# A decoder layer in fp32: the first softmax sum of a differential head moved into the RMS norm's factor, and the sliding pairs' values moved behind their transposes

## The chip, the cores and the metric

The kernel runs on one core of a Trainium2 chip. The metric is the device time of one execution in microseconds (us), as a median over runs. The engines are named as in the profile: PE is TensorE (PEld its weight loads), DVE VectorE, ACT ScalarE, POOL GpSimd, and SP is SyncE, which issues most of the DMAs. A line such as L766 is line 766 of the kernel before.

## What is computed

One layer, width 1024, 512 tokens, all in fp32. A conditioned RMS norm and one input projection feed two causal mixers side by side: sliding-window attention (8 heads, a sink per head) and differential attention (4 heads). Each mixer is projected to the width, gated and merged; an output projection, a second norm, a gated MLP with a short convolution and a final norm follow. The change touches the two mixers:

```python
# differential attention, one block of 128 queries
p = jax.nn.softmax(scores, axis=-1)
a = p[:, :, 0] - lam * p[:, :, 1]
out = jnp.einsum('bhqs,bshe->bqhe', a.astype(v.dtype), v)
...
out = _rmsnorm(out, subln_g) * (1.0 - lam_init)

# sliding window: softmax over 256 keys and one sink, then the values
probs = jax.nn.softmax(jnp.concatenate([scores, sink], axis=-1), axis=-1)[..., :-1]
out = jnp.einsum('bnkgqs,bnskd->bnqkgd', probs.astype(v.dtype), vb)
```

## The kernel before, in words

**Products.** An fp32 matrix product is made of three matmuls on operands split in a high and a low part (mm3, L121 to L124). Whoever makes an operand casts the high part on ScalarE and subtracts it on VectorE to get the low part (evac, L490 and L491, or with a scale L493 and L494; for weights split, L118 and L119).

**Stages.** Up to about 56 us the input projection of the sliding heads; then the sliding heads to about 111 us; the differential heads with the first gates to about 215; more gates and the merge to about 310; then the output projection and the MLP (L1260, L1875) to the end.

**Fills.** While softmax work runs on VectorE and ScalarE, TensorE is kept busy with *fill* steps (L539): each takes one k-step, three matmuls of 128x512, of the next unit in a list. The units are the q, k and v projections of the differential heads (add_head, L679), and the gates and branch projections. Their weights are loaded by SyncE two units ahead (load_cols, L519) into four shared "raw" buffers. The values of a differential head are transposed on TensorE in a turn that comes V_LAG = 13 fills after their projection (pv, L703).

**The w_ada rows.** In the same raw buffers VectorE sums up rows of the conditioning matrix: loads of 512 KB (ada_load, L828), each multiplied and added by two L852 (the first of a row by L850) into arow, and every 8th fill takes one more step of it (ada_rows, L832). For two of these steps (ROW_BEHIND) the sum may only be issued behind the division of a given sliding pair. A finished row is spread over the partitions by TensorE (pr, L869).

**PSUM.** Eight banks: two "f" for the projections, three "s" for scores, two "t" for transposes and anything short (tp, td, pv, pr, pss, rb, and the values oa of sliding pairs 0, 1 and 3), one "v" (oa of pair 2, the od of differential heads, some score tiles). The t bank goes in turns, so whoever takes one waits until the last but one user has been read.

**Order.** TensorE's order is the program's (a manual schedule). The order on VectorE and ScalarE is found by a scheduler from priorities (high_priority) and "issue after" conditions, before the program runs; at run time each engine then works strictly in its order.

**Sliding pairs.** Two heads are worked together (i and i+4): four pairs. Per pass of the loop at L928: SWA_FILL[3] = 2 fills; the values of pair i−1 (swa_values, L661) and the scores of pair i+1; the transposes of pair i for head j=0, first half (four, tile tp), one fill, second half (three), one fill; those for j=1 (seven in a row); two fills; the softmax of pair i+1 (L620 to L644); five fills. The values of pairs 2 and 3 come behind the loop.

**Differential heads.** A loop over 16 steps s, one per head and block of 128 queries: fills, scores of two steps ahead (sd, L742), transposes of the finished step (diff_transpose, td, L778), softmax of the two steps ahead (diff_softmax, L749), and behind each head its values (diff_values, od) and statistics. In the softmax ScalarE makes the exponentials of both maps and their sums (L760); VectorE takes the reciprocals (L763), multiplies the second with −lambda (L764), scales the second map by it (L765) and adds the first map scaled by its own reciprocal (L766). From od the squares are summed over channels by TensorE (pss, L801), the norm's factor is made (rstd_m2, L178 to L195), turned by a transpose (rb, L808) and multiplied in, NORM_LAG = 16 fills later for the last head and in a later step for the others.

Of the kernel before, what the change touches and what calls it, by code (L numbers as in the profile page):

```python
# [8 lines left out]
F32 = mybir.dt.float32  # L9
F32R = mybir.dt.float32r  # L10
AF = mybir.ActivationFunctionType
ALU = mybir.AluOpType
PSUM = bass.MemoryType.PSUM

P = 128
# [3 lines left out]
NT = S // P  # L19
# [19 lines left out]
SWA_FILL = (2, 2, 5, 2, 2, 2, 2, 3)  # L39
DIFF_FILL = (3, 2, 4, 2)  # L40
# [14 lines left out]
def kernel(  # L55
# [22 lines left out]
    nc = tc.nc  # L78
# [21 lines left out]
    def tbank(name, shape=(P, S)):  # L100
        return bank("t", 2, list(shape), name)

    def vbank(name):
        return bank("v", 1, [P, S], name)
# [92 lines left out]
    def rstd_m2(dst, ssq, n, d, wpool, plus=None):  # L197
        rstd_end(dst, *rstd_start(ssq, n, d, wpool, plus), n, wpool)
# [242 lines left out]
    for gi in range(KT):  # L441
# [4 lines left out]
        else:  # L446
            h_low(gi)
            lp = cpool.tile([P, 2, 64], F32, name="lp")
            ls = cpool.tile([P, 2], F32, name="ls")
            nlam = cpool.tile([P, 1], F32, name="nlam")  # L450
# [31 lines left out]
    ap = pool("att", stack=at)  # L482
# [56 lines left out]
    def fill(n):  # L539
        for _ in range(n):  # L540
            if not current:
                prefetch()
                if loaded:
                    wts, run = loaded.pop(0)
                    current.append(run(wts))
                    if tick[0]:
                        prefetch()
            if tick[0] == 7:
                prefetch()
            if current:  # L550
                try:
                    next(current[0])
                except StopIteration:
                    current.clear()
            for e in list(later):
                e[0] -= 1
                if e[0] <= 0:
                    later.remove(e)
                    e[1]()
            tick[0] += 1  # L560
            if tick[0] >= ADA_START and tick[0] % ADA_EVERY == 0:
                next(ada, None)
# [6 lines left out]
    def flush(*kinds):  # L569
        for kind in kinds:  # L570
            while beside[kind]:
                beside[kind].pop(0)()
# [70 lines left out]
                    sb = c.sb[n][:, j, :w]  # L643
                    c.divided = nc.vector.tensor_scalar_mul(sb, sb, c.lsum[:, j, n : n + 1])  # L644

    def swa_transpose(i, j, halves=(0, 1)):
        c = pairs[i]
        if 0 in halves:
            c.pT.append(ap.tile([P, 1024], F32, tag="aTh" if j == 0 else "aTl", bufs=2, name=f"pT{i}_{j}"))
        pt = c.pT[j]  # L650
        for b in halves:
            wb = 512 if b == 0 else 384
            tp = tbank(f"tp{i}_{j}_{b}")
            for m in range(wb // P):
                kb, n = 2 * b + m // 2, 2 * b + m // 2 + m % 2
                off = (kb - max(0, n - 1)) * P
                nc.tensor.transpose(tp[:, m * P : (m + 1) * P], c.sb[n][:, j, off : off + P], ident)
            with tc.high_priority(offset=HP):
                c.copied = nc.scalar.copy(pt[:, b * 512 : b * 512 + wb], tp[:, :wb])

    def swa_values(i):  # L661
        o = vbank(f"oa{i}") if i == 2 else tbank(f"oa{i}")
        for kb in (0, 2, 1, 3):
            w = P if kb == 3 else 2 * P
            for j in range(2):
                rows = slice(64 * j, 64 * j + 64)
                nc.tensor.matmul(
                    o[rows, kb * P : kb * P + w], va[:, kb, rows],
                    pairs[i].pT[j][:, kb * 256 : kb * 256 + w],
                    start=kb == 0, stop=kb == 3, tile_position=(0, 64 * j),  # L670
                )

        with tc.high_priority(offset=HP), tc.issue_after(pairs[3].divided.ins) if i == 2 else ExitStack():
            evac(outa[0][:, i], outa[1][:, i], o)
# [74 lines left out]
    def diff_softmax(*ss):  # L749
        with tc.high_priority(offset=HP):  # L750
            for s in ss:
                nc.vector.tensor_scalar_mul(scored[s][0], scored[s][0], -(2.0 ** (-2 * (s // NT + 1))))  # L752
            behind = ExitStack()
            for s in ss:
                h, n = divmod(s, NT)
                slope = 2.0 ** (-2 * (h + 1))
                mx, pm = scored[s]
                lsum = ap.tile([P, 2], F32, tag="dls", bufs=3, name=f"dls{h}_{n}")
                for m in range(2):
                    exp = nc.scalar.activation(  # L760
                        pm[m], pm[m], AF.Exp, bias=mx[:, m : m + 1], scale=slope, accum_out=lsum[:, m : m + 1]
                    )
                nc.vector.reciprocal(lsum, lsum)  # L763
                nc.vector.tensor_mul(lsum[:, 1:2], lsum[:, 1:2], nlam)  # L764
                nc.vector.tensor_scalar_mul(pm[1], pm[1], lsum[:, 1:2])  # L765
                last = nc.vector.scalar_tensor_tensor(pm[0], pm[0], lsum[:, 0:1], pm[1], ALU.mult, ALU.add)  # L766
                probs[s] = pm[0]
                behind.enter_context(tc.issue_after(exp.ins))
                behind.enter_context(tc.issue_after(last.ins))
            behind.close()  # L770
# [12 lines left out]
    def diff_values(h):  # L783
        t, (aTh, aTl) = heads[h], aTs[h]
        o = vbank(f"od{h}")
        for k in range(NT):
            q0 = k * P
            mm3(
                o[:, q0:], t[:, 4, k * P : (k + 1) * P], t[:, 5, k * P : (k + 1) * P],
                aTh[:, k * AW + q0 : k * AW + 512], aTl[:, k * AW + q0 : k * AW + 512],  # L790
                k == 0, k == NT - 1,
            )
        sq = ap.tile([P, S], F32, tag="tmp", bufs=2, name=f"sq{h}")
        of = ap.tile([P, S], F32, tag="of", bufs=2, name=f"of{h}")
        nc.scalar.activation(sq, o, AF.Square)
        nc.scalar.activation(of, o, AF.Copy, scale=sublnc)

        def stats():
            pss = tbank(f"pss{h}", (P, NT))
            for n in range(NT):  # L800
                nc.tensor.matmul(pss[:, n : n + 1], sq[:, n * P : (n + 1) * P], ones[:, 0:1], start=True, stop=True)  # L801
            rs = ap.tile([P, NT], F32, tag="drs", bufs=2, name=f"drs{h}")
            rstd_m2(rs, pss, NT, P, ap)

            def turn_norm():
                rb = tbank(f"rb{h}")
                for n in range(NT):
                    nc.tensor.transpose(rb[:, n * P : (n + 1) * P], rs[:, n : n + 1].to_broadcast([P, P]), ident)  # L808
                nc.vector.tensor_mul(of, of, rb)
                split(outd[0][:, h], outd[1][:, h], of)  # L810

            if h < 3:
                beside["norm"].append(turn_norm)
            else:
                after(NORM_LAG, turn_norm)

        if h < 3:
            beside["sum"].append(stats)
        else:
            after(STAT_LAG, stats)  # L820
# [86 lines left out]
        units.append((lambda: load_cols(win, COL_GA + j * P, f"wga{j}"), gate))  # L907
        units.append((load, branch))

    group_ahead = [1]  # L910
    pairs, firsts, scored, probs, aTs = {}, {}, {}, {}, {}
    ada = ada_rows()
    add_head(0)
# [14 lines left out]
    for i in range(SWA_PAIRS):  # L928
        more = i + 1 < SWA_PAIRS
        fill(SWA_FILL[3])  # L930
        if more:
            flush("row")
            if i:
                swa_values(i - 1)
            swa_scores(i + 1, range(NT))
        swa_transpose(i, 0, (0,))
        fill(1)
        swa_transpose(i, 0, (1,))
        fill(SWA_FILL[4] - 1)
        swa_transpose(i, 1)  # L940
        fill(SWA_FILL[5])
        if more:
            with tc.issue_after(pairs[i].copied.ins):
                swa_softmax(i + 1)
        fill(SWA_FILL[6] + SWA_FILL[7])
    while units or loaded or current:
        fill(1)
    flush("row")
# [9 lines left out]
    fill(DIFF_FILL[0])  # L958
    for s in range(4 * DIFF_HEADS):
        h, n = divmod(s, NT)  # L960
        if n == 0 and 0 < h < 3:
            add_head(h + 1)
        elif s == 12:
            add_gate_a(2)
            add_gate_a(3)
        fill(DIFF_FILL[1])
        nxt = (s + 1, s + 2) if n % 2 and s < 15 else ()
        if nxt:
            flush("row")
            diff_scores(*nxt)  # L970
        if n == 1:
            diff_transpose(s)
        fill(DIFF_FILL[2])
        if n == 2:
            flush("sum")
        elif n == 0:
            flush("norm")
        if n != 1:
            diff_transpose(s)
        if s == 13:  # L980
            group_ahead.clear()
        elif s > 13:
            flush("row")
        diff_softmax(*nxt)
        if n == 0 and h:
            diff_values(h - 1)
            fill(DIFF_FILL[3])
# [334 lines left out]
    ssq, r2, xns = {}, {}, {}  # L1322
# [608 lines left out]
```

## Time and profile before

| | us |
|---|---|
| median of 3 runs | 693.56 (693.17 to 693.79) |
| the profiled execution's own time | 693.12 |
| its span in the trace | 691.1 |
| TensorE busy | 679.9 of 691.1 |
| VectorE busy | 567.8 |
| ScalarE busy | 383.9 |

All groups of lines below are of the profiled execution, in us from the start of its span. Busy time is a sum over stages; what an engine's wait is worth is read where it stands, in the timeline. In a timeline row stand the start, the length, the engine, the line, the operation, what it writes and reads, the shapes and how many of them follow each other; a bracket gives the idle time before the row and who ended it. Rows of TensorE overlap: matmuls are pipelined.

### The profile page before, as it was taken

Reading aid. Unit: us, or ns where it says so; the run is one execution under the profiler, and the core shown is the slowest. Engines: PE = TensorE matmul, PEld = TensorE weight load, DVE = VectorE, ACT = ScalarE, POOL = GpSimd, SP = SyncE. Lnnn points to the kernel's source line nnn. Section 1 sums busy time; section 2 is a strip of 40 time slices with the busy share of each in tenths; the row PEclk is TensorE's granted clock in tenths of the full one; section 3 lists DMA queues with packets and bytes.
Section 4 is the critical chain, followed back from the end, with each engine's and each line's share of the span. In section 5 each row is a group of like instructions: output and inputs, shape, how many; then the busy total and the mean of one; then the engine's idle time right before and its main releaser. Section 6 shows DMA issues by size and latency. Waiting matters only on the chain.

```text
span 691.1 us, 11254 instructions
## 1 busy us (share of the span) xinstructions
PE 679.9 (98%) x4203; PEld 592.9 (86%) x4203; DVE 567.8 (82%) x1073; ACT 383.9 (56%) x686; POOL 83.3 (12%) x100
## 2 busy tenths in 40 slices
PE   8999999999999999999999999999999999999995
PEld 5887787778888888888899999999999999888884
DVE  4999996987985666663789988888888999979997
ACT  6676675445552323332477756655565666656665
POOL 3000000000101000000030101112111002540300
PEclk9999999999999999999999999999999999999998
DMA  9985454553456675229725788777889648996903
GB/s 304 350 241 178 151 156 126 154 159 97 140 143 181 195 219 178 91 96 308 236 60 125 169 211 199 164 174 215 189 227 223 155 155 202 193 203 193 167 1 121
DMA packets 115926, 121.81 MB, mean 176 GB/s; under 512 B 4447, under 2 KB 93344, under 8 KB 115872
## 3 DMA queue, kind: packets, MB, share of 16 engines
q1 hardware_dynamic: 96958, 95.09, 43.3%
q0 software_dynamic: 18720, 25.73, 21.9%
q8 instruction: 33, 0.54, 0.3%
q10 hardware_dynamic: 194, 0.28, 0.1%
q14 instruction: 21, 0.17, 0.1%
HBM read 118.97 MB, written 2.11 MB: 175 GB/s over the span
## 4 chain that ended last, share of the span: by engine, by line
PE 89%; DVE 5%; DMA 3%; issue 1%; ACT 1%; SPq 0%; POOLq 0%; ACTq 0%
PE up L1260 32%; PE dc L1875 15%; PE a L385 5%; DMA ra<-in_w_ada_dram 2%; PE pgd L122 2%; PE oc L1316 2%; PE oc L1320 2%; PE pgd L124 2%; PE oc L1317 2%; PE pgd L123 2%; PE pga L122 2%; PE pga L124 2%; PE pga L123 2%; DVE arow L852 1%; PE pB L122 1%; PE pB L123 1%
## 5 line engine op out<-in xcount | busy, mean ns | idle before, releaser
L1260 PE MATMUL up<-t,m_whi 128*128 128x256 f32 x512 | 93.1, 283 | 0.0
L1260 PEld LDWEIGHTS up<-t,m_whi 128*128 128x128 f32 x512 | 79.9, 192 | 0.0
L1260 PE MATMUL up<-t,m_wlo 128*128 128x256 f32 x256 | 72.4, 283 | 0.0
L1260 PE MATMUL up<-bh,p_whi 128*128 128x256 f32 x232 | 65.7, 283 | 0.0
L1260 PE MATMUL up<-bl,p_whi 128*128 128x256 f32 x232 | 65.7, 283 | 0.0
L1260 PE MATMUL up<-bh,p_wlo 128*128 128x256 f32 x232 | 65.7, 283 | 0.0
L852 DVE SCALAR_TENSOR_TENSOR arow<-ra,cs,arow 128x512 f32<-128x512 f32 x56 | 41.9, 749 | 14.9 <-DMA ra<-in_w_ada_dram 14.2
L1260 PEld LDWEIGHTS up<-t,m_wlo 128*128 128x128 f32 x256 | 49.2, 192 | 0.0
L1260 PEld LDWEIGHTS up<-bh,p_whi 128*128 128x128 f32 x232 | 44.5, 192 | 0.0
L1260 PEld LDWEIGHTS up<-bl,p_whi 128*128 128x128 f32 x232 | 44.5, 192 | 0.0
L1260 PEld LDWEIGHTS up<-bh,p_wlo 128*128 128x128 f32 x232 | 44.5, 192 | 0.0
L1169 POOL DMA_DIRECT2D s<-in_w_up_dram x21 | 27.1, 1366 | 141.0 <-DMA s<-in_w_up_dram 62.9
L1197 ACT CAST m_whi<-s 128x1024 fp32r<-128x1024 f32 x31 | 32.4, 1047 | 11.1 <-DVE s L1191 7.7
L1201 DVE TENSOR_TENSOR m_wlo<-s,m_whi 128x1024 fp32r<-128x1024 f32 x31 | 37.7, 1217 | 0.0
L1260 PE MATMUL up<-t,p_whi 128*128 128x256 f32 x176 | 32.2, 283 | 0.0
L875 POOL DMA_DIRECT2D mod_rows<-row x8 | 5.0, 622 | 207.1 <-ACT row L874 207.1
L185 POOL TENSOR_TENSOR r<-ms,mhalf 128x1 f32<-128x1 f32 (+1 forms) x16 | 13.8, 865 | 117.2 <-DVE ms L183 72.9
L1260 PEld LDWEIGHTS up<-t,p_whi 128*128 128x128 f32 x176 | 27.5, 192 | 0.0
L1267 ACT ACTIVATE gT<-a,cv 128x512 f32<-128x512 f32 x22 | 17.7, 813 | 16.9 <-DVE a L1302 15.8
L1197 ACT CAST p_whi<-wa 128x1024 fp32r<-128x1024 f32 x18 | 18.8, 1042 | 12.6 <-PE up L1260 12.6
L760 ACT ACTIVATE sd<-sd,dmx 128x128 f32<-128x128 f32 (+3 forms) x32 | 17.6, 554 | 13.5 <-DVE dmx L752 13.3
L1201 DVE TENSOR_TENSOR p_wlo<-wa,p_whi 128x1024 fp32r<-128x1024 f32 x18 | 22.0, 1221 | 3.8 <-ACT p_whi L1197 3.8
(488 smaller groups left out, 2074.4 us busy)
## 6 DMA issues: line engine op xcount, KB each, us to landing
ra<-in_w_ada_dram SPq DMA_DIRECT2D x32, 512.0 KB, 3.7
wa<-in_w_up_dram SPq DMA_DIRECT2D x22, 512.0 KB, 4.2
s<-in_w_up_dram SPq DMA_DIRECT2D x21, 512.0 KB, 4.7
s<-in_w_up_dram POOLq DMA_DIRECT2D x21, 512.0 KB, 7.2
adaw<-in_w_ada_dram SPq DMA_DIRECT2D x12, 512.0 KB, 7.0
w<-in_w_in_dram SPq DMA_DIRECT2D x12, 512.0 KB, 4.7
a<-in_w_up_dram SPq DMA_DIRECT2D x11, 512.0 KB, 4.5
b<-in_w_down_dram SPq DMA_DIRECT2D x10, 512.0 KB, 5.3
```

The costliest lines, as they stand in the source:

```text
L122: nc.tensor.matmul(o, lh, rh, start=start, stop=False)
L123: nc.tensor.matmul(o, lh, rl, start=False, stop=False)
L124: nc.tensor.matmul(o, ll, rh, start=False, stop=stop)
L385: nc.tensor.matmul(acc6[i], lhs[:, i * P : (i + 1) * P], rhs[k], start=k == 0 and p == 0, stop=last and p == 2)
L760: exp = nc.scalar.activation(pm[m], pm[m], AF.Exp, bias=mx[:, m : m + 1], scale=slope, accum_out=lsum[:, m : m + 1])
L852: nc.vector.scalar_tensor_tensor(ac, r[:, a], cc, ac, ALU.mult, ALU.add)
L1169: nc.gpsimd.dma_start(dst, upblock(*blk), accum_op=ALU.add)
L1197: nc.scalar.copy(W[J, name][0], R[J, SRC[name]])
L1201: nc.vector.tensor_sub(lo, R[J, SRC[name]], hi.bitcast(F32))
L1260: nc.tensor.matmul(o[u], w[:, k, cu], b[:, k], start=name in ("p1", "m5", "p2") and k == 0 and x == 0, stop=k == 3 and x == 2, skip_group_ ...
L1267: nc.scalar.activation(grow(j), av[J][:, u], AF.Identity, bias=cv[:, 66 + j : 67 + j], scale=cv[:, 44 + j : 45 + j])
L1875: nc.tensor.matmul(bank2[u][:, sl], a[:, q, cu], b[:, q, sl], start=first_mm and x == 0, stop=last_mm and x == 2, skip_group_check=name no ...
```

## The change

Four things.

1. swa_transpose does both halves of a head at once. For j=0 the fill that stood between the halves now stands behind them.
2. The values of pairs 0 and 1 are taken in their own pair's pass, behind SWA_FILL[6] = 2 fills that follow the transposes, and no longer ahead of the next pass's scores: five fills earlier. All values but those of pair 3 use the v bank.
3. The differential softmax no longer divides by the first map's sum. With s0 and s1 the sums of the two maps, it makes e0 + (−lambda·s0/s1)·e1, which is s0 times what it made before. The sixteen L765 go, L763 and L764 act on one column, and L766 reads the same two maps. What is left of s0 goes into the norm's factor: with r = 1/s0 the sum of squares is multiplied by r² ahead of the norm's epsilon, and the factor by r. These are four operations on 128x4 per head. The sums of a head's four blocks are kept in one tile for that.
4. In step s = 1 of the differential loop one fill moves from ahead of the scores and the transposes to behind them. (The condition at add_head is written anew and means the same.)

The loads, their order on SyncE and the number of matmuls stay.

```diff
-    def swa_transpose(i, j, halves=(0, 1)):
+    def swa_transpose(i, j):
         c = pairs[i]
-        if 0 in halves:
-            c.pT.append(ap.tile([P, 1024], F32, tag="aTh" if j == 0 else "aTl", bufs=2, name=f"pT{i}_{j}"))
-        pt = c.pT[j]
-        for b in halves:
+        pt = ap.tile([P, 1024], F32, tag="aTh" if j == 0 else "aTl", bufs=2, name=f"pT{i}_{j}")
+        c.pT.append(pt)
+        for b in range(2):
...
     def swa_values(i):
-        o = vbank(f"oa{i}") if i == 2 else tbank(f"oa{i}")
+        o = tbank(f"oa{i}") if i == 3 else vbank(f"oa{i}")
...
-                lsum = ap.tile([P, 2], F32, tag="dls", bufs=3, name=f"dls{h}_{n}")
-                for m in range(2):
+                if n == 0:
+                    sums[h] = ap.tile([P, 2, NT], F32, tag="dls", bufs=2, name=f"dls{h}")
+                ls0, ls1 = (sums[h][:, m, n : n + 1] for m in range(2))
+                for m, ls in enumerate((ls0, ls1)):
                     exp = nc.scalar.activation(
-                        pm[m], pm[m], AF.Exp, bias=mx[:, m : m + 1], scale=slope, accum_out=lsum[:, m : m + 1]
+                        pm[m], pm[m], AF.Exp, bias=mx[:, m : m + 1], scale=slope, accum_out=ls
                     )
-                nc.vector.reciprocal(lsum, lsum)
-                nc.vector.tensor_mul(lsum[:, 1:2], lsum[:, 1:2], nlam)
-                nc.vector.tensor_scalar_mul(pm[1], pm[1], lsum[:, 1:2])
-                last = nc.vector.scalar_tensor_tensor(pm[0], pm[0], lsum[:, 0:1], pm[1], ALU.mult, ALU.add)
+                nc.vector.reciprocal(ls1, ls1)
+                nc.vector.scalar_tensor_tensor(ls1, ls1, ls0, nlam, ALU.mult, ALU.mult)
+                last = nc.vector.scalar_tensor_tensor(pm[0], pm[1], ls1, pm[0], ALU.mult, ALU.add)
...
-            rs = ap.tile([P, NT], F32, tag="drs", bufs=2, name=f"drs{h}")
-            rstd_m2(rs, pss, NT, P, ap)
+            rs, r0, r2 = (ap.tile([P, NT], F32, tag=t, bufs=2, name=f"{t}{h}") for t in ("drs", "dr0", "dr2"))
+            nc.vector.reciprocal(r0, sums[h][:, 0])
+            nc.vector.tensor_mul(r2, r0, r0)
+            nc.vector.tensor_mul(r2, r2, pss)
+            rstd_m2(rs, r2, NT, P, ap)
+            nc.vector.tensor_mul(rs, rs, r0)
...
         if more:
             flush("row")
-            if i:
-                swa_values(i - 1)
             swa_scores(i + 1, range(NT))
-        swa_transpose(i, 0, (0,))
-        fill(1)
-        swa_transpose(i, 0, (1,))
-        fill(SWA_FILL[4] - 1)
+        swa_transpose(i, 0)
+        fill(SWA_FILL[4])
         swa_transpose(i, 1)
         fill(SWA_FILL[5])
         if more:
             with tc.issue_after(pairs[i].copied.ins):
                 swa_softmax(i + 1)
-        fill(SWA_FILL[6] + SWA_FILL[7])
+        fill(SWA_FILL[6])
+        if i < 2:
+            flush("row")
+            swa_values(i)
+        fill(SWA_FILL[7])
...
-        fill(DIFF_FILL[1])
+        ahead = s == 1
+        fill(DIFF_FILL[1] - ahead)
         nxt = (s + 1, s + 2) if n % 2 and s < 15 else ()
         if nxt:
             flush("row")
             diff_scores(*nxt)
         if n == 1:
             diff_transpose(s)
-        fill(DIFF_FILL[2])
+        fill(DIFF_FILL[2] + ahead)
```

More of the change, by code (lines that the diff above doesn't have):

```diff
@@ L908, in add_gate_a @@
         units.append((load, branch))
-    group_ahead = [1]
+    group_ahead, sums = [1], {}
     pairs, firsts, scored, probs, aTs = {}, {}, {}, {}, {}
@@ L960 @@
         h, n = divmod(s, NT)
-        if n == 0 and 0 < h < 3:
+        if s in (4, 8):
             add_head(h + 1)
```

## The prediction

> **What bounds the kernel now.** I read the page first: its row of the granted clock and its chain of waits.
>
> ```profile
> PEclk9999999999999999999999999999999999999998
> ...
> PE 89%; DVE 5%; DMA 3%; issue 1%; ACT 1%; SPq 0%; POOLq 0%; ACTq 0%
> ```
>
> TensorE runs at full clock from end to end and holds 89% of the chain that ended last, so a part of this change counts only as far as it makes TensorE wait less or more. Next came the table of stretches, for the part of the program that the change touches.
>
> ```profile
> 83.00:108.00 25.00, 25.00 (x160) 20.26 (x162) 20.15 (x73) 18.12 (x54) 0.00 (x0) 1.00 0.49 147
> ```
>
> Its first pair of numbers is the stretch's length and TensorE's busy time: 25.00 of 25.00 us. There is nothing to win here, but a new wait would cost its full length. The view of TensorE's waits and its timeline then give the stalls that can be won. Here are all of them above 0.3 us between 56 and 683 us, each with the row ahead of it (columns: start, length, instruction; in brackets the idle time before it and what ended it).
>
> ```profile
> 81.28 0.40 PE L124 MATMUL pw<-hThB,w_l 128*128 128x512 f32 x1
> 82.57 0.55 PE L657 MATMUL tp<-ident,st 128*128 128x128 f32 x3 [0.89 <-DVE outal L491]
> ```
>
> ```profile
> 128.61 0.39 PE L122 MATMUL pA<-outah,wba_h 128*128 128x512 f32 x1
> 128.84 0.39 PE L123 MATMUL pA<-outal,wba_h 128*128 128x512 f32 x1
> 129.07 0.39 PE L124 MATMUL pA<-outah,wba_l 128*128 128x512 f32 x1
> 129.85 0.52 PE L778 MATMUL td<-ident,sd 128*128 128x128 f32 x3 [0.40 <-DVE dls L763]
> ...
> 138.07 0.39 PE L124 MATMUL pq<-hThA,w_l 128*128 128x512 f32 x1
> 138.81 0.30 PE L778 MATMUL td<-ident,sd 128*128 128x128 f32 x1 [0.35 <-DVE dls L763]
> ```
>
> Matmuls follow each other at 0.23 us (128.61, 128.84, 129.07), so a fill step of three takes 0.69. TensorE would have been free at 81.28 + 0.23 = 81.51, 129.30 and 138.30. The three stalls are so 1.06, 0.55 and 0.51 us; the brackets are shorter because a matmul's row overlaps the next one's. The first is tp1_0_1 waiting for a t bank that oa0 held until VectorE had made outal from it. The other two are td0_2 and td1_0 waiting for the softmax (the bracket names L763; L766, the last of that group, is what the transposes read).
>
> **The sliding pairs.** (1) oa0 moves to the v bank, so the stall before tp1_0_1 goes: −1.06 us. (2) The step that stood between the two halves of j=0 now stands behind them. That makes the second half due one fill earlier, and its t bank may not be free. For pairs 1 and 2 it is: it held transposes that ScalarE has copied long before. For pair 3 the bank of tp3_0_1 was that of pv0, the values of the first differential head behind their transposes, and it comes free only when VectorE has done L491 on pv.
>
> ```profile
> 104.69 0.49 PE L657 MATMUL tp<-ident,st 128*128 128x128 f32 x3
> ...
> 105.72 0.93 PE L657 MATMUL tp<-ident,st 128*128 128x128 f32 x7
> ```
>
> ```profile
> 91.59 1.22 DVE L119 TENSOR_TENSOR wga_l<-wga,wga_h 128x1024 fp32r<-128x1024 f32 x1
> 92.72 0.68 DVE L494 SCALAR_TENSOR_TENSOR qkv<-pq,qkv 128x512 fp32r<-128x512 f32 x1
> 93.33 0.68 DVE L491 TENSOR_TENSOR outal<-oa,outah 128x512 fp32r<-128x512 f32 x1
> 93.92 0.74 DVE L852 SCALAR_TENSOR_TENSOR arow<-ra,cs,arow 128x512 f32<-128x512 f32 x1
> 94.58 0.28 DVE L620 CUSTOM_DVE_ANT_0 st<-sw,dsw 128x128 f32<-128x128 f32 x1
> ...
> 97.07 0.36 DVE L631 TENSOR_SCALAR nm<-mx,nsink 128x4 f32<-128x4 f32 x2
> ...
> 103.36 0.69 DVE L491 TENSOR_TENSOR qkv<-pv,qkv 128x512 fp32r<-128x512 f32 x1
> ```
>
> Before, VectorE ended at 103.36 + 0.69 = 104.05, and tp3_0_1, at 104.69, didn't wait. Now TensorE comes to it 1.06 earlier by the stall that went, and 0.78 earlier by the fill that moved (1.03 from 104.69 to 105.72 holds one fill and the three transposes; a fill's first matmul behind transposes costs 0.09 more): at about 102.85. Even at before's VectorE times that is a wait of 1.2 us.
>
> And VectorE gets later, not earlier. outal of oa1 is now done long before (it was at 93.33; it fits into idle time and shifts the rest little), and the new order of VectorE's instructions puts the first L852 on ra01_4 *ahead* of wga's L119, which with L494 stood ahead of it. VectorE executes in order, so wga's L119, L494, the scores of pair 3, their softmax and L491 on pv are all queued behind a wait for that load. Its row on SyncE, the DMA view's median for the two issued between 86 and 94 us, and, for the line's four issues between 86 and 100 us, the least, median and longest from issue to landing:
>
> ```profile
> 88.53 4.67 SPq L828 DMA_DIRECT2D ra<-in_w_ada_dram  x2
> ```
>
> ```profile
> ra<-in_w_ada_dram SPq DMA_DIRECT2D x2, 512.0 KB, 4.8
> ```
>
> ```profile
> DMA to landing us min/median/max: 3.7/4.3/4.8
> ```
>
> The order of SyncE's issues and what they wait for is unchanged, and the buffer that ra01_4 takes comes free by VectorE work whose sum ahead of it is the same. So I leave its issue at 88.53 and take 4.8: landed at 93.33. VectorE would be free for it about 1.3 us sooner (my estimate: 93.92 less outal's 0.59, wga's and qkv's 1.74 and what is added ahead, about 0.5 for outal and a later sum of the softmax). From 93.33: L852 0.66 (93.92 to 94.58) gives 93.99; L119 1.13 (91.59 to 92.72) 95.12; L494 0.61, 95.73; the scores 2.49 (94.58 to 97.07), with the second L852, 0.66, now among them, 98.88. What follows on ScalarE was queued in before behind copies of the transposes:
>
> ```profile
> 97.70 0.31 ACT L632 ACTIVATE es<-nm,sink 128x4 f32<-128x4 f32 x1
> ```
>
> That is 0.63 behind VectorE's 97.07; with the copies out of the way I take VectorE's row of 0.36 instead: 99.24. From there to L491 on pv were 5.66 us (97.70 to 103.36), all of it exponentials and what hangs on them: 104.90, its 0.69, and 0.14 of signal (an L766 that ended at 129.09 + 0.62 released TensorE at 129.85; its row is below): TensorE goes on at **105.73**, a new stall of 2.9 us. From there to the next seven transposes it has 1.03 and the moved fill's 0.69: 107.45 against 105.72 before. **The sliding part: +1.73 us** (1.06 won, 2.79 lost). Its bounds are 104.05 + 0.14 + 1.72 = 105.91 (+0.2) if VectorE were no later than before, and, with a load 1.1 us slower again (4.8 less 3.7, put on top), +2.8. I take the middle, as it adds up from rows.
>
> (3) The values moved by five fills, the same 16 matmuls, and a fill's saving of 0.09 where transposes were merged against one where values now part two fills, cancel. All of it lies ahead of that stall, which absorbs up to 2.9 us; so nothing. pr00, oa2 and oa3, and the gates behind them, shift as one.
>
> **The differential heads.** Sixteen L765 go (0.42 at 384 columns). Instead each head has four operations on 128x4 (nothing above 0.36, the row of two such at 97.07; I take 0.2 each), and L764 gets a third operand at one column.
>
> ```profile
> 122.16 0.44 PE L778 MATMUL td<-ident,sd 128*128 128x128 f32 x2
> ```
>
> ```profile
> 120.65 0.35 DVE L765 TENSOR_SCALAR sd<-sd,dls 128x256 f32<-128x256 f32 x1
> 120.91 0.68 DVE L491 TENSOR_TENSOR qkv<-pv,qkv 128x512 fp32r<-128x512 f32 x1
> 121.51 0.47 DVE L766 SCALAR_TENSOR_TENSOR sd<-sd,dls,sd 128x256 f32<-128x256 f32 x1
> ...
> 128.63 0.42 DVE L765 TENSOR_SCALAR sd<-sd,dls 128x384 f32<-128x384 f32 x1
> 129.09 0.62 DVE L766 SCALAR_TENSOR_TENSOR sd<-sd,dls,sd 128x384 f32<-128x384 f32 x1
> ...
> 137.99 0.29 DVE L765 TENSOR_SCALAR sd<-sd,dls 128x128 f32<-128x128 f32 x1
> 138.31 0.35 DVE L766 SCALAR_TENSOR_TENSOR sd<-sd,dls,sd 128x128 f32<-128x128 f32 x1
> ```
>
> In before's times: td0_1 comes one fill earlier, at 122.16 − 0.69 = 121.47. L766 takes L765's place, and L491 on pv1, whose bank td0_1 needs, follows: 120.65 + 0.39 + 0.69 = 121.73, with 0.14 TensorE goes at 121.87: a new stall of 0.40, which carries to td0_2 (the fills between are one more): arrival 129.70. Its data, without L765's 0.46 (128.63 to 129.09): 129.85 − 0.46 = 129.39. So no wait; the gain is 0.15. td1_0 then arrives at 138.15. Its L766 had ended at 138.66; ahead of it three L765 go (0.46 for that of 128.63, at least as much for the next block's with 512 columns, 0.32 for its own from 137.99 to 138.31) and two of the small operations come (0.4): 138.66 − 1.24 + 0.4 + 0.14 = 137.96, no wait. The gain grows to 138.81 − 138.15 = **0.66 us**. If only its own L765 counted, 138.81 − 0.32 = 138.49 would leave a gain of 0.32; and nothing, if an exponential comes last. A fourth stall, some 0.1 us ahead of td2_2, goes too by my estimate. The final factor's two operations lengthen the path from pss to rb by 0.4 to 0.8; NORM_LAG puts 16 fills (11 us) between, which hide it.
>
> **Sum:** 1.73 − 0.66 − 0.1 = about +0.95 us on the profiled execution's 693.12, 694.07. That execution lies 0.44 under the median of 693.56, so I expect a median of **694.5**.
>
> **Rivals.**
> *The load doesn't bind.* With 3.7 us from issue to landing the chain to L491 comes 1.1 earlier, and the sum is 0.95 − 1.1 = −0.15: 693.4. Were the bank of tp3_0_1 free on time altogether, it would be 693.56 − 1.06 − 0.76 = 691.7. For it: 3.7 stands in the row; only VectorE's order, not a need of data, puts wga behind ra01_4. Against it: 4.8 is the time for that very transfer, and even before's 104.05 is 1.2 too late.
> *The differential part gives nothing (slower).* The two stalls, before td0_2 and td1_0, end where they ended before if ScalarE's exponentials, and not VectorE's operations behind them, come last. Its place is VectorE at 128.63 and 138.31, its price the 0.66, and it decides as soon as L766 ends no earlier although L765 is gone. Then only +1.73 stands: 695.3. For it: the small operations wait for the exponentials, too. Against it: L765 stands between them and L766 in the rows above.
> *A slow clock behind the new stall.* 2.9 us idle could lower the granted clock for the matmuls that follow. If it halved for as long as the idle time, half of 2.9 us would be lost: 1.45, so 694.5 + 1.45 = 696.0. It decides only if a stall of that length is long enough. The PEclk row is 9 through the stall of 1.06, which speaks against it but is shorter. [...]
> *It doesn't do what it says for the time:* bank and stall trade evenly, 693.6.
>
> **How the numbers follow.** Forecast 0.48. Load early or no net effect 0.18 (of which 0.09 at 691.7 or near). Differential part nothing, or a longer wait on the bank, 0.28. Slow clock 0.06. About 0.2%, 1.39 us, can be told from no change: 692.17 to 694.95. Faster: 0.09 and a little of the forecast's spread, 0.1. Slower: 0.28 + 0.06, 0.34, less what the differential part gives in part and more for the forecast's own spread (medians here lie within 0.3 us): 0.35. The range runs from 692.3 (between 691.7 and the early load) to 695.8 (sliding part +1.73, 0.5 more on the bank); outside stay the slow clock and most of the fully free bank.
>
> **What would show it.** In the changed profile: no idle before tp1_0_1 near 81; L852 on arow waiting for DMA ra near 92 to 93 us on VectorE; tp3_0_1 idle 2 to 3 us near 103, released by qkv's L491; td0_1 with 0.4 behind the same line; no stalls before td0_2 and td1_0. If tp3_0_1 waits less than 1 us, or if TensorE past 240 us shows idle time of its own, the forecast is wrong.

## The result, and the profile after

| | before | with the change |
|---|---|---|
| median (20 runs each) | 693.59 us | 695.38 us |
| lowest to highest | 693.04 to 695.18 | 694.03 to 698.0 |
| ratio, 95% interval | | 1.0025 (1.0017 to 1.0033) |
| profiled execution, its span | 693.12, 691.1 | 695.87, 693.8 |

The change makes the kernel 1.8 us slower. The forecast was 694.5, in a range of 692.3 to 695.8: the side and the place were right, and about half of the loss is missing. The executions also scatter twice as far as before.

TensorE's waits with the change, as total, times, longest (the change shifts the lines: L657 is now L656, L852 is L856, L828 is L832, and L764 to L766 are the three VectorE operations that are left of the softmax; in the experiments the lines shift by a few once more):

```profile
PE tp L656 <- DVE qkv L491: 2.1, 1, 2.1
...
PE td L778 <- DVE qkv L491: 0.2, 1, 0.2
```

The wait of tp on outal and the two of td on dls are gone. In their place stand two waits on L491 of qkv, both forecast. The timeline of VectorE shows where the long one is made:

```profile
91.34 1.07 DVE L644 TENSOR_SCALAR st<-st,lsum 128x128 f32<-128x128 f32 x4
93.36 0.75 DVE L856 SCALAR_TENSOR_TENSOR arow<-ra,cs,arow 128x512 f32<-128x512 f32 x1 [0.94 <-DMA ra<-in_w_ada_dram]
94.03 1.22 DVE L119 TENSOR_TENSOR wga_l<-wga,wga_h 128x1024 fp32r<-128x1024 f32 x1
...
98.91 0.36 DVE L631 TENSOR_SCALAR nm<-mx,nsink 128x4 f32<-128x4 f32 x2
...
104.87 0.68 DVE L491 TENSOR_TENSOR qkv<-pv,qkv 128x512 fp32r<-128x512 f32 x1
```

VectorE idles for 0.94 us on the load of ra01_4, with wga's product (L119) in line behind it, and comes to L491 on pv at 104.87. TensorE's timeline around that:

```profile
102.89 0.60 PE L656 MATMUL tp<-ident,st 128*128 128x128 f32 x4
105.61 0.55 PE L656 MATMUL tp<-ident,st 128*128 128x128 f32 x3 [2.12 <-DVE qkv L491]
105.92 0.48 PE L122 MATMUL pw<-hThA,w_h 128*128 128x512 f32 x1
106.23 0.59 PE L123 MATMUL pw<-hTlA,w_h 128*128 128x512 f32 x1
106.62 0.63 PE L124 MATMUL pw<-hThA,w_l 128*128 128x512 f32 x1
107.05 0.63 PE L122 MATMUL pw<-hThA,w_h 128*128 128x512 f32 x1
...
107.90 0.63 PE L124 MATMUL pw<-hThA,w_l 128*128 128x512 f32 x1
108.33 1.59 PE L656 MATMUL tp<-ident,st 128*128 128x128 f32 x7
109.67 0.48 PE L122 MATMUL pw<-hThB,w_h 128*128 128x512 f32 x1
```

Read the starts. In before, the three matmuls of a fill behind transposes start 0.32, 0.23 and 0.23 us apart. Here they start 0.31 and 0.39 us apart, from 106.62 on 0.43, and the seven transposes take 1.34 (108.33 to 109.67), where before they took 0.68 (105.72 to 106.40). After that the pace is as before. The table of stretches has the reason; its last but two column is the granted clock:

```profile
105.60:106.50 0.90, 0.89 (x5) 0.85 (x6) 0.55 (x1) 0.30 (x1) 0.00 (x0) 0.87 0.00 0
106.50:107.50 1.00, 1.00 (x4) 0.71 (x4) 0.00 (x0) 0.17 (x1) 0.00 (x0) 0.50 0.00 0
107.50:108.50 1.00, 1.00 (x4) 0.70 (x3) 0.00 (x0) 0.00 (x0) 0.00 (x0) 0.50 0.05 16
108.50:109.50 1.00, 1.00 (x7) 1.00 (x6) 0.00 (x0) 0.03 (x1) 0.00 (x0) 0.50 0.00 0
109.50:111.00 1.50, 1.50 (x9) 1.20 (x7) 0.00 (x0) 0.94 (x2) 0.00 (x0) 0.94 0.00 0
```

A mean of 0.87 over 0.90 us means that the last 0.23 us ran at half clock (0.13 × 0.90 / 0.5), and 0.94 over 1.50 that the first 0.18 did: TensorE ran at half speed from 106.27 to 109.68, for 3.41 us, and lost 1.7 us of work. The page's row of the granted clock, in slices of 17 us, is the same as before's and hides this. (The 8 at its end stands in both. It is the time behind TensorE's last matmul, which in before starts at 683.48: there the stretch from 688 to 691 us has 0.50. So "full clock from end to end" in the prediction holds up to that point only, and even an undisturbed execution has a mean of about 0.997.)

### The profile page after: what moved, and what is told of

Its sections match the earlier page's. It is cut to its first block, busy times and chain, and to the rows that moved or that the text cites. A ratio compares the mean times of both kernels' runs of the same rounds, so it can differ in the third digit from the quotient of the medians.

```text
span 693.8 us, 11248 instructions
## 1 busy us (share of the span) xinstructions
PE 681.7 (98%) x4203; PEld 594.1 (86%) x4203; DVE 565.4 (81%) x1073; ACT 383.7 (55%) x686; POOL 82.0 (12%) x100
## 5 line engine op out<-in xcount | busy, mean ns | idle before, releaser
L856 DVE SCALAR_TENSOR_TENSOR arow<-ra,cs,arow 128x512 f32<-128x512 f32 x56 | 42.0, 750 | 19.3 <-DMA ra<-in_w_ada_dram 18.5
```

What stands on the lines that cost most here:

```text
L856: nc.vector.scalar_tensor_tensor(ac, r[:, a], cc, ac, ALU.mult, ALU.add)
```

## The experiments

**Theory.** Three terms make the result: (1) the differential part gives about 0.75 us; (2) the sliding part costs about 1.7 us through the wait of tp3_0_1 on L491 of pv, which the load of ra01_4 in VectorE's order makes longer; (3) that wait, in some executions and not in others, is followed by one stretch of 3.4 us at half clock, 1.5 to 1.7 us more. **Rivals:** the differential part gives nothing; the half clock has another cause; L491 is late for another reason than the load's place; what is won ahead of tp3 is lost again ahead of td.

Every execution has a mean granted clock on record beside its time. One stretch of 3.4 us at half clock is 3.4 × 0.5 / 693 = 0.0025 of it. None of the 78 executions of before that ran beside the experiments has less than 0.996; so 0.995 or less marks an execution with such a stretch.

### The two parts alone

The sliding part alone is the full change without the parts in diff_softmax, the statistics and step 1 (a part of the diff, from the full change to this run):

```diff
...
-                nc.vector.reciprocal(ls1, ls1)
-                nc.vector.scalar_tensor_tensor(ls1, ls1, ls0, nlam, ALU.mult, ALU.mult)
-                last = nc.vector.scalar_tensor_tensor(pm[0], pm[1], ls1, pm[0], ALU.mult, ALU.add)
+                nc.vector.reciprocal(lsum, lsum)
+                nc.vector.tensor_mul(lsum[:, 1:2], lsum[:, 1:2], nlam)
+                nc.vector.tensor_scalar_mul(pm[1], pm[1], lsum[:, 1:2])
+                last = nc.vector.scalar_tensor_tensor(pm[0], pm[0], lsum[:, 0:1], pm[1], ALU.mult, ALU.add)
...
```

> The sliding part alone (merged halves, earlier values, v bank), with the differential softmax as before. Theory: the sliding part costs 1.7 us at full clock, by the wait of tp3_0_1 on qkv's L491, and 1.6 to 1.7 us more in an execution whose clock record holds a window at half speed behind that wait; the differential part gives back 0.75 us in the full change. So this kernel takes about 695.3 us without such a window and 697.0 with one, a median 0.6 to 0.9 above the full change. Rival: the differential part gives nothing, and this kernel equals the full change (695.4).

The differential part alone keeps those parts and takes back swa_transpose, swa_values and the loop over the pairs (again a part, from the full change):

```diff
...
-        swa_transpose(i, 0)
-        fill(SWA_FILL[4])
+        swa_transpose(i, 0, (0,))
+        fill(1)
+        swa_transpose(i, 0, (1,))
+        fill(SWA_FILL[4] - 1)
...
```

> The differential part alone (sixteen L765 gone, the sums in the norm's factor, one fill moved in step 1), with the sliding pairs as before. Theory: the stalls ahead of td0_2 and td1_0 and the small one ahead of td2_2 go, a wait of 0.4 us ahead of td0_1 comes: 0.75 us faster than before, 692.85. Rival: the exponentials come last, no change (693.6). The stall of 1.06 us ahead of tp1_0_1 stays in both, and the granted clock behind it stays full.

On one chip, with before at 693.82: the sliding part alone 695.81, ratio 1.0034 (1.0023 to 1.0046); the differential part alone 693.06, ratio 0.9992 (0.9982 to 1.0002). So the first costs 2.0 us and the second gives about 0.8; the second's interval just includes no change, so that its size rests on the trace as well. TensorE's timeline of the differential part alone, at td0_2:

```profile
129.27 0.39 PE L124 MATMUL pA<-outah,wba_l 128*128 128x512 f32 x1
129.53 0.52 PE L779 MATMUL td<-ident,sd 128*128 128x128 f32 x3
```

No wait, and 0.32 us earlier than before's 129.85. Among its waits none of td on the softmax is left:

```profile
PE td L779 <- DVE qkv L491: 0.2, 1, 0.2
```

In the sliding part alone both waits of td on the softmax stand as before, and two more, shorter ones come on its L765 (L766 of before):

```profile
PE tp L656 <- DVE qkv L491: 2.6, 1, 2.6
...
PE td L777 <- DVE dls L762: 0.8, 2, 0.4
PE td L777 <- DVE sd L765: 0.5, 2, 0.3
```

That is where this part's cost lies in its profile: the seven transposes behind the wait start at 107.54 (reckoned from the row ahead of them at 106.85, with three matmuls at 0.23), 1.8 us later than before's 105.72, as the prediction had it (1.73), and the first of the two new waits, ahead of td0_1, takes about 0.35 more. The rival that the differential part gives nothing falls. Of the sliding part's six executions four had a full clock (0.996), at 695.6 to 695.9, which is 1.8 to 2.1 above before's median; two had 0.994, at 696.7 and 697.4. The expected 695.3 at full clock was 0.3 too low.

### TensorE kept at work during the wait

```diff
         for b in range(2):
             wb = 512 if b == 0 else 384
+            if (i, j, b) == (3, 0, 1):
+                busy = sbank("busy")
+                for _ in range(8):
+                    nc.tensor.matmul(busy, hTh[0][:, :P], hTh[0], start=True, stop=True)
             tp = tbank(f"tp{i}_{j}_{b}")
```

> The full change with eight extra matmuls of 128x512 (1.9 us, into a PSUM bank that nobody reads) between the two halves of pair 3, where TensorE otherwise idles 2.4 us waiting for qkv's L491. Nothing else moves. Theory of the clock: the idle time, not the wait, lets the granted clock fall to half for one window; with TensorE at work the clock stays full, tp3_0_1 starts at the same 105.6, and the time falls to that of the full change's executions without a slow window, 694.3 to 695.0, none above 695.5. Rival: the half clock comes from something else, and the time stays at 695.4 with executions above 696.

It was run twice, the second time beside the full change:

> The full change with the eight extra matmuls in pair 3's wait, beside the full change. Theory: no execution at 0.995 or less; the time is that of the full change's executions at 0.997, 694.3 to 695.3, and the median lies 0.5 to 1.5 us below the full change's. Rival: the same time as the full change.

> The full change, run beside the next kernel for more executions of both on one chip. Theory: executions with a mean granted clock of 0.995 or less (one window of 3.4 us at half speed is 0.0025 of the span) take 1.0 to 1.7 us more than those at 0.997 or above; median 695.4 to 696.4, by how many of them fall in. Rival: clock and time are not related.

| | median | ratio to before (95%) | executions at 0.995 or less |
|---|---|---|---|
| full change, beside the second run | 696.03 | 1.0034 (1.0022 to 1.0047) | 6 of 11 |
| with extra matmuls, first run | 695.05 | 1.0019 (1.0010 to 1.0028) | 0 of 11 |
| with extra matmuls, second run | 695.13 | 1.0021 (1.0012 to 1.0030) | 0 of 11 |

In the timeline of the second run tp3_0_1 starts no earlier than in the full change:

```profile
103.32 2.11 PE L655 MATMUL busy<-hThA 128*128 128x512 f32 x8
106.01 0.55 PE L660 MATMUL tp<-ident,st 128*128 128x128 f32 x3 [0.58 <-DVE qkv L491]
106.31 0.48 PE L122 MATMUL pw<-hThA,w_h 128*128 128x512 f32 x1
106.63 0.40 PE L123 MATMUL pw<-hTlA,w_h 128*128 128x512 f32 x1
```

It goes at 106.01, the full change in its own profile at 105.61. With eight matmuls whose result nobody reads, the median lies 0.9 us below the full change's beside it. The two intervals overlap, so the time alone doesn't settle it; the count of executions at 0.995 or less does: 0 of 22 against 6 of 11 beside them, and 20 of 37 in all. Filling the idle time keeps the clock full behind the wait, though the wait still ends where it did. The full change scatters because its executions come in two groups. Over all three of its runs here (20 of the result, 6 and 11 beside the experiments), 20 of 37 executions are at 0.995 or less, with a median of 696.26; 14 are at 0.997, with a median of 694.74; the other three have 0.996, and with them, as some executions of before have 0.996 too, the median at full clock is 694.97. So the half clock costs 1.3 to 1.5 us where it happens.

The expected "none above 695.5" was too sharp: in the first run three executions lay at 695.65 to 696.62, in the second four at 695.53 to 695.96, all at full clock. Before has such late executions at full clock as well (695.78 is its latest here). What makes them late is not the half clock behind tp3_0_1. One of them can be read: the profiled execution of the first run (696.62, 1.6 above its run's median) has a granted clock of 1.00 in every stretch from 102 to 110 us. What does make them late is not shown.

A further run of the full change alone gave the same picture on another chip:

> The full change once more, on the same chip as the next two, to compare them with. Theory: about half of its executions hold a window at half clock behind the wait of tp3_0_1 (mean granted clock 0.995 or less) and take 695.6 to 696.9; the others take 694.0 to 695.3. Median 695.4. Rival: clock and time are not related.

Its median is 696.36, ratio 1.0039 (1.0024 to 1.0053), with five of six executions at 0.995 or less (696.2 to 698.1) and one at 0.997 (693.82).

### A shorter wait

The fill of pair 3 goes back between the halves of j=0:

```diff
...
         for b in range(2):
             wb = 512 if b == 0 else 384
+            if b:
+                fill(between)
             tp = tbank(f"tp{i}_{j}_{b}")
...
-        swa_transpose(i, 0)
-        fill(SWA_FILL[4])
+        swa_transpose(i, 0, int(i == 3))
+        fill(SWA_FILL[4] - (i == 3))
```

> The full change, but with pair 3's fill put back between the two halves of j=0. The wait of tp3_0_1 shrinks from 2.4 to about 1.6 us and ends at the same 105.6, and what follows comes one fill earlier: 0.78 us less than the full change at equal clock, so about 693.8 at full clock. Whether 1.6 us of idle time is enough for a slow window is open: if so, executions with it take 695.4; if not, none shows a half clock and the spread is that of before.

Measured: 695.62 us, ratio 1.0020 (1.0010 to 1.0030), in two clean groups. Five executions at full clock took 693.66 to 694.57 (median 694.08), six at 0.995 or less 695.62 to 697.2. The profiled one had a full clock, with this wait:

```profile
103.44 0.40 PE L124 MATMUL pw<-hThA,w_l 128*128 128x512 f32 x1
105.72 0.55 PE L658 MATMUL tp<-ident,st 128*128 128x128 f32 x3 [1.88 <-DVE qkv L491]
```

From 103.44 + 0.23 to 105.72 it is 2.05 us long, not 1.6, and it is enough for the half clock in about half of the executions. Shorter stalls were not: not the 1.06 us ahead of tp1_0_1 in before (none of 78), and not the 1.45 us at the same place in the profile of the differential part alone (from 81.10 to 82.55; none of its 11).

### The load's place in VectorE's order

```diff
                 hold = tc.issue_after(pairs[sorted(pairs)[ROW_BEHIND[k]]].divided.ins)
+                if k == 4:
+                    behind_wga = tc.issue_after(splits[-3][1].ins)
...
-            with hold:
+            with hold, (behind_wga if idx == 0 and hf == 1 and k == 4 else ExitStack()):
```

This puts both multiplications on ra01_4 behind wga's L119 and qkv's L494, and the second of them behind the scores too.

> The full change, with the two multiplications on ra01_4 (L856) put behind wga's L119 and qkv's L494 again in VectorE's order. Theory: VectorE then does those 1.7 us of work while the load is under way; the scores of pair 3 start 0.9 us earlier, L491 on pv too (103.9), and the wait of tp3_0_1 shrinks from 2.4 to about 1.4 us: 0.9 us less than the full change at full clock, 694.1, and fewer or no slow windows, so a median 1.0 to 1.5 below. Rival: the load's place doesn't decide (L491 on pv is late for another reason); no change, 695.4.

Measured: 692.57 us, ratio 0.9992 (0.9982 to 1.0003), 3.8 us below the full change on the same chip, and none of 11 executions at 0.995 or less. VectorE's timeline:

```profile
91.92 1.22 DVE L119 TENSOR_TENSOR wga_l<-wga,wga_h 128x1024 fp32r<-128x1024 f32 x1
93.05 0.69 DVE L494 SCALAR_TENSOR_TENSOR qkv<-pq,qkv 128x512 fp32r<-128x512 f32 x1
93.65 0.75 DVE L858 SCALAR_TENSOR_TENSOR arow<-ra,cs,arow 128x512 f32<-128x512 f32 x1
...
96.80 0.36 DVE L631 TENSOR_SCALAR nm<-mx,nsink 128x4 f32<-128x4 f32 x2
...
102.77 0.68 DVE L491 TENSOR_TENSOR qkv<-pv,qkv 128x512 fp32r<-128x512 f32 x1
```

L491 on pv comes at 102.77, 2.1 us earlier than with the change, and the view of waits has 0.4 for TensorE where it had 2.1. The gain was expected at 0.9 and is 2.1: the expectation left out that the second multiplication, too, went out of the scores (0.67), and this execution was 0.4 ahead from the start. The rival falls: the place of two instructions in an order makes most of the wait. (Reckoned from the end of the last transpose ahead of it, as below, the wait falls from 2.4 to 0.65.)

### Other banks for pair 3

```diff
-            tp = tbank(f"tp{i}_{j}_{b}")
+            tp = (sbank if i == 3 and (j, b) != (0, 0) else tbank)(f"tp{i}_{j}_{b}")
```

> The full change, with the last three transpose tiles of pair 3 in the s banks (free since the scores of pair 3 were read) in place of the t banks. Nothing else moves. Theory: no tile of pair 3 waits for L491 on pv any more; TensorE saves all of the wait, reaches the last seven transposes at 105.0 (before: 105.72, full change: 108.33), no slow window, and the gain of the differential part, 0.75, stands: 692.2, up to 692.9 if the chain over pr and the loads of ra behind it keeps a part. That would be faster than both. Rival: what is won there is lost ahead of td0_1 or td0_2, which wait for VectorE and the loads; 693.5.

Measured: **692.28 us, ratio 0.9982 (0.9973 to 0.9990)**: faster than before by 1.1 us, as expected, and the interval excludes no change; none of 11 executions is at 0.995 or less. Against the full change it is 4.1 us on the same chip, where five of that one's six executions had the half clock, and 2.5 against its executions at full clock (694.74). TensorE's and VectorE's timelines:

```profile
103.17 0.99 PE L656 MATMUL tp<-ident,st 128*128 128x128 f32 x7
103.92 0.48 PE L122 MATMUL pw<-hThA,w_h 128*128 128x512 f32 x1
```

```profile
105.65 0.68 DVE L491 TENSOR_TENSOR qkv<-pv,qkv 128x512 fp32r<-128x512 f32 x1
```

L491 on pv is as late as ever, even later, and no transpose of pair 3 waits for it: the seven follow each other without a stop. Ahead of td TensorE waits 0.3 us in all, 0.1 more than in the full change, so what is won is not lost again there. Both edits together:

> The s banks for pair 3's last three transpose tiles and the two multiplications on ra01_4 behind wga's L119, together. Theory: the banks alone have taken the whole wait already; what VectorE now does earlier helps only the 0.3 us that is left ahead of td0_1: 692.0 to 692.3, not to be told from the banks alone (692.3). Rival: the chain over pr and the gates' loads gains too, 691.5.

They took 692.12, ratio 0.9984 (0.9975 to 0.9992), not to be told from the banks alone, again with no execution at 0.995 or less.

## Why the prediction was right, and where its size was off

- **The stall ahead of tp1_0_1 goes:** right. No wait on outal is left.
- **A new wait of tp3_0_1 on pv's bank:** right in place, in cause and nearly to the tenth in its end. ra01_4 was worked out to land at 93.33, VectorE took it up at 93.36; nm 99.24 less 0.36, that is 98.88, measured 98.91; L491 at 104.90, measured 104.87; TensorE's start at 105.73, measured 105.61. A part of this closeness is luck. The load was issued at 88.85, 0.32 later than taken over from before, and took 4.5 us from issue to landing and not 4.8; the two errors cancel:

```profile
88.85 9.16 SPq L832 DMA_DIRECT2D ra<-in_w_ada_dram  x3
```

```profile
ra<-in_w_ada_dram SPq DMA_DIRECT2D x1, 512.0 KB, 4.5
```

- **Its length:** 2.9 us forecast, 2.4 measured (from 102.89 + 0.35 to 105.61). TensorE came to it later than worked out: of the 1.06 us won ahead of tp1_0_1 only 0.67 had arrived there (102.89 against 103.56 in before). That takes nothing off the cost, since the end is set by VectorE.
- **The load as the cause:** right, shown by the order with the multiplications put later, which takes most of the wait away.
- **The differential part, −0.66 and −0.1:** right. td0_1 waits (0.2 for 0.4 forecast), td0_2 and td1_0 don't, and the part alone measures −0.8, with an interval of −1.2 to +0.1.
- **The sum, +0.95:** at full clock the change costs 694.74 − 693.5, about 1.2 us by the medians, or 1.5 with the executions at 0.996 (694.97); that is 0.3 to 0.5 more than forecast. The two profiled executions agree better: their spans differ by 2.7 us (693.8 and 691.1), and without the 1.7 lost at half clock 1.0 is left. What the medians have on top is not taken apart.
- **The range, 692.3 to 695.8:** that the result's 695.38 lies in it is in part luck. The range was made without the half clock, and in that run 9 of 20 executions had it; in the two later runs of the same kernel it was 5 of 6 and 6 of 11, and their medians, 696.36 and 696.03, lie above the range.
- **"A slow clock behind the new stall", chance 0.06, 696.0:** this is the step that failed, the weight that it got. It is no alternative to the forecast: it falls on about half of the executions (20 of 37), and so it shifts the median by part of its price and doubles the scatter. Its price came out nearly right (1.45 us; measured 1.3 to 1.5 by the medians, 1.7 in the profiled execution), but by luck: the prediction let the half clock last as long as the idle time, 2.9 us, while it lasted 3.4 behind an idle time of 2.4. What before's trace shows is that its stall of 1.06 us leaves the clock full (1.00 from 81 to 86 us); it has no longer one between 56 and 683 us, so how much idle time is needed it could not tell. Here 2.4 us were enough, with 3.41 us at half clock behind them (106.27 to 109.68), and the shorter wait, 2.05 us in its profiled execution, which kept its clock, was followed by half clock in 6 of 11.

Why the same wait halves the clock in one execution and not in the next is not shown. Two traces show that the clock fell at different times against the release of TensorE. In the further run of the full change the clock fell before TensorE was released, not behind it:

```profile
105.97 0.90 PE L656 MATMUL tp<-ident,st 128*128 128x128 f32 x3 [2.58 <-DVE qkv L491]
```

```profile
105.00:106.00 1.00, 0.03 (x1) 0.03 (x1) 1.00 (x4) 0.23 (x1) 0.00 (x0) 0.68 0.00 0
106.00:108.00 2.00, 2.00 (x7) 1.71 (x8) 0.52 (x1) 0.48 (x1) 0.00 (x0) 0.50 0.00 0
108.00:109.00 1.00, 1.00 (x4) 0.76 (x3) 0.00 (x0) 0.00 (x0) 0.00 (x0) 0.62 0.00 0
```

That is from 105.36 to 108.76, again 3.40 us, 0.6 ahead of the release at 105.97; in the profile of the result it fell 0.66 us behind the release. In the sliding part alone the same wait of 2.6 us ended with the clock full:

```profile
103.00:106.00 3.00, 0.42 (x4) 0.23 (x3) 2.37 (x9) 2.02 (x7) 0.00 (x0) 1.00 0.31 119
106.00:108.00 2.00, 2.00 (x14) 1.70 (x13) 0.31 (x1) 0.48 (x1) 0.00 (x0) 1.00 0.00 0
```

What sets these executions apart no run here shows, so this stays open.

## What to carry to other kernels

When an edit makes TensorE come earlier to a shared PSUM bank, look up who holds that bank and when its reader is done: the win of one wait became a longer one, and three tiles in other banks turned a loss of 0.25% into a gain of 0.18%. VectorE, which worked in its order, met a load early here, idled 0.94 us on it with wga's product in line, and came to L491 on pv 2.1 us later than with the two multiplications put behind that product (104.87 against 102.77). So read the new order of every engine, not only that of the one that was edited. And where an edit gives TensorE a new idle time as long as those here (2.05 to 2.6 us), price the half clock behind it too, in a share of the executions; the mean granted clock of each execution shows it (0.995 or less, and never below 0.996 in before) where the page's row does not.

## What the runs showed of the hardware

One idle stretch of 2.05 to 2.6 us on TensorE (lengths in the profiled executions) was followed, in 20 of 37 executions of the full change, 6 of 11 with the shorter wait and 2 of 6 of the sliding part, by half clock (a mean of 0.995 or less). In two traces of the full change it lasted 3.41 and 3.40 us; there it cost 1.3 to 1.5 us by the medians. Stalls of 1.06 us (78 executions) and 1.45 us (11) never were. Idle time filled with eight matmuls that compute nothing of use kept the clock up in 22 of 22 executions; the median was 0.9 us lower, within overlapping intervals.
